# One loaded mask for all branches, an early read of the largest count, and a first gate unit that is split for crowded experts

## The chip, the cores and the metric

One core of a Trainium2 chip runs the whole program. The metric is device time in microseconds (us) of one launch. Engines: PE (TensorE, matmuls), DVE (VectorE), ACT (ScalarE), POOL (GpSimd), SP (here the issuer of the weight loads). Each runs its own instructions in order.

## The reference

Two post-norm layers over 256 positions of width 1024. Each layer has a mixer (spatial gating beside gated linear attention) and a feed-forward; the second layer's is a mixture of 8 experts, of which each position takes two.

```python
def gla_chunked(q, k, v, log_a):          # chunks of 64 positions, 4 heads
    ...
    scores = jnp.where(causal, jnp.einsum('nbhid,nbhjd->nbhij', q_dec, k_inv), 0.0)
    o_intra = jnp.einsum('nbhij,nbhje->nbhie', scores, v)
    ...
def swiglu(x, w_gate, w_up, w_down):
    return (jax.nn.silu(x @ w_gate) * (x @ w_up)) @ w_down

def moe_swiglu(x, w_router, e_gate, e_up, e_down):    # 8 experts, 1024 -> 3584 -> 1024
    logits = (t @ w_router).astype(jnp.float32)
    top_val, top_idx = lax.top_k(logits, TOP_K)
    top_w = jax.nn.softmax(top_val, axis=-1)
    gates = jnp.sum(jax.nn.one_hot(top_idx, N_EXPERTS, dtype=jnp.float32) * top_w[..., None], axis=1)
    out = jnp.zeros_like(t)
    for e in range(N_EXPERTS):
        out = out + gates[:, e:e + 1] * swiglu(t, e_gate[e], e_up[e], e_down[e])
```

All tensors are float32.

## The kernel before, in words

**Precision.** A float32 matmul is made of faster passes in F32R, a format with fewer bits that TensorE reads in one go: ACT copies an operand to its high part `h`, DVE subtracts to get the low part `l` (the helper `split`, lines 263 and 264). A product is `h·h + l·h + h·l`. A matmul of unsplit float32 operands needs no split, and takes two instructions in the trace for each one in the program.

**Weights.** Expert weights come as units of 1 MB: 128 partitions x 2048 float32. The loop over experts `e` takes columns in groups `g`, one of 512 and three of 1024 (group 3 is the last). A group of 1024 has four gate units `eg` (u0 to u3), four up units `eu`, and four down units `ed`, 12 loads. The class `Stream` keeps a ring of slots of one unit: a load takes a slot for `r`, a split takes two more for `h` and `l` and gives back `r`'s, and `free` gives back the rest once the product has read them. `tick()` stands for a step of the program's time: it lets the side tasks go on (a task that yields 4 goes on four ticks later) and pumps the stream, that is, issues the loads for which slots are free and the splits that are due. The order of each engine's instructions is the order in which this Python code emits them.

**Few and many.** Each expert gathers its positions into up to 128 columns. With 64 or fewer, the high parts stand in columns 0 to 63 and the low parts in 64 to 127, so that one pass does two, and the passes with `exl` or `cle` are left out. The choice is a branch on PE, ACT and DVE: `Expert.cases` (line 952) tests the expert's count, which `nc.values_load` (line 890) has read into a register of each of the three engines, once for each of the 8 experts. An expert with more than 64 positions is called a many expert below, the others few experts.

**The unsplit unit.** The first gate unit u0 of every group but the very first is not split. Its 4 matmuls (8 instructions, line 1033) multiply the raw weights `r` by `xw`, an unsplit copy of half of the gathered positions, for many and few experts alike. One `tick()` stands before each of the four.

**Side tasks that fall in this unit.** In the last group of an expert the next expert's gather starts: `one_hot` on DVE (lines 962 to 969), then four ticks, then `gather`: two transposes on PE (line 995), the first pick (8 matmuls in the program, line 983), its split `exh` (lines 974, 975), and two ticks later the second pick. In the second group of an expert the last one's `scatter` starts: two splits (`yh`, `yl`), three ticks, two pairs of matmuls (lines 1145, 1146) for the first half, two ticks, two pairs for the second half.

**Elsewhere.** In the mixer, the attention product of the first 128 positions is written as two matmuls of 64 columns for each head (line 640). At the end of the program, line 1226 reads the largest count of an expert, and line 1227 branches on it: a loop for counts over 128, which is jumped over here.

Of the kernel before, what the change touches and what calls it, by code (L numbers as in the profile page):

```python
# [8 lines left out]
F32 = mybir.dt.float32  # L9
# [30 lines left out]
def trunk(ctx: ExitStack, tc: tile.TileContext, x, w_in, gm_ws, gm_bs, gm_ln_g, gm_ln_b, gla_wa2, gla_ba,  # L40
# [86 lines left out]
    class Stream:  # L127


        def __init__(self):  # L130
            self.plan, self.index, self.parts, self.raw, self.held = [], {}, {}, {}, {}
            self.loaded = self.split = self.freed = 0
            self.whole = set()
# [5 lines left out]
        def add(self, key, src, a, b, pieces=1, ticks=4, whole=False):  # L139

            self.index[key] = len(self.plan)
            if whole:
                self.whole.add(self.index[key])
            self.plan.append((src, a, b, pieces, self.at))
            self.at += ticks

        def cols(self, key, w, c0, n, pieces=(1, 1), ticks=None, whole=()):
            v = w[:, c0:c0 + n].rearrange("(k p) n -> p k n", p=P)
            kk = 2048 // n
            for u in range(KT // kk):  # L150
                self.add((*key, u), v[:, u * kk:u * kk + kk, :], kk, n, pieces[u] if kk > 2 else 1, ticks or kk,
                         u in whole)
# [23 lines left out]
        def converting(self):  # L176
            i = self.split
            src, a, b, pieces, _ = self.plan[i]
            if i == self.loaded:
                self.load()  # L180
            r, slot = self.raw.pop(i)
            if i in self.whole:
                self.parts[i] = r, None
                self.held[i] = slot,
                self.split += 1
                return
            h, sh = self.slot(f"h{i}", F32R, a, b)
            l, sl = self.slot(f"l{i}", F32R, a, b)
# [275 lines left out]
    def mixer(l, xT, small, ready, nxT):  # L464
# [70 lines left out]
        def attention():  # L535
# [98 lines left out]
            for tb in range(2):  # L634
                yield 6
                po = psy(f"o{l}{tb}", (P, H, P))
                for h in range(H):
                    p, hh = divmod(h, 2)
                    for r in (slice(0, 64), slice(64, P)) if tb == 0 else (slice(0, P),):
                        nc.tensor.matmul(po[r, h, :], scT[tb][:, h, r], vs[tb][:, h * P:(h + 1) * P], start=True,  # L640
                                         stop=tb + r.start == 0)
                    for c in (2 * tb, 2 * tb + 1):
                        if c > 0:
                            r = slice(64 * (c % 2), 64 * (c % 2) + 64)
                            nc.tensor.matmul(po[r, h, :], qbd[tb][:, p, hh, r], S[c][:, p, :], start=False, stop=True)
# [136 lines left out]

    def moe_plan():
        prev = None
        for e in range(NE):
            for g, (c0, n) in enumerate(groups(e)):
                W.cols(("eg", e, g), exp_g[0, e], c0, n, ticks=4, whole=(0,) if e + g else ())
# [12 lines left out]
    def moe_constants():  # L800
# [9 lines left out]
        nc.vector.tensor_tensor(pair, ident[0:2 * NE, 0:NE], ident[0:2 * NE, NE:2 * NE], op=ALU.add)  # L810

        fold = const.tile([P, HALF], F32, name="fold")
        nc.vector.tensor_tensor(fold, ident[:, 0:HALF], ident[:, HALF:P], op=ALU.add)
        return iota, pri, one.to_broadcast([P, P]), ecst, pair, fold

    def moe(xT, ready, consts):
        iota, pri, ones, ecst, pair, fold = consts
# [33 lines left out]
        load_i = const.tile([P, NE], I32, name="load_i")  # L851
# [3 lines left out]
        def routing():  # L855
# [78 lines left out]
        class Expert:  # L934
# [7 lines left out]
            def __init__(self, nm, rank, gate, fewer=None):  # L942
                self.nm, self.rank, self.gate, self.fewer = nm, rank, gate, fewer
                self.load = None
                self.hT = {}

            def cases(self, few, many):

                if self.load is None:
# [41 lines left out]
            def gather(self):  # L991
# [9 lines left out]
                for hf in range(2):  # L1001
# [3 lines left out]
                    if hf == 0:  # L1005
                        if self.load is not None:
# [11 lines left out]
            def product(self, units, n, nm):  # L1018
# [6 lines left out]
                for u, ((wh, wl), free) in enumerate(units):  # L1025
                    held.append(free)
                    for j in range(kk):
                        k = kk * u + j
                        for b in range(nb):
                            s = slice(b * 512, b * 512 + 512)  # L1030
                            tick()
                            if wl is None:
                                nc.tensor.matmul(p[b], self.xw[:, k, :], wh[:, j, s], start=k == 0, stop=False,  # L1033
                                                 skip_group_check=True)
                                continue
# [13 lines left out]
                return p  # L1049

# [107 lines left out]


# [66 lines left out]
        most = nc.values_load(cnt_i[0:1, 0:1], min_val=0, max_val=2 * P)  # L1226
# [154 lines left out]
```

## Time and profile before

| | us |
|---|---|
| median of 3 runs | 1357.31 (1356.94 to 1363.91) |
| the profiled execution | 1356.93 |
| its span | 1355.2 |
| PE busy | 1295.6 (96%) |
| DVE busy | 1066.6 (79%) |
| ACT busy | 842.0 (62%) |
| DMA queue of the weights, share of 16 engines | 80.1% |

The span is what the trace covers, from its first instruction to its last; 1.7 us of the execution lie around it. A row of a timeline gives start, duration, engine, line, operation, output and inputs, and how many instructions it joins; in brackets the idle time of the engine before it and what ended that. PE and PEld are matmuls and weight loads of TensorE; a name with a q (PEldq, DVEq) is an engine's sequencer: loads of registers, branches, semaphores.

### The profile page before, as it was taken

The numbers are of one execution on the slowest core, as the hardware profiler recorded it, in microseconds if no ns is written. First come the engines' busy times: TensorE is split into PE (matmuls) and PEld (weight loads), VectorE is DVE, ScalarE is ACT, GpSimd is POOL, SyncE is SP. The second block draws the span as 40 slices with busy tenths as digits, with TensorE's granted clock in tenths as the row PEclk, the third lists the DMA queues.
The fourth block names the chain that finished last, engine by engine and source line by source line (L and its number), as shares of the span: only waits on it lengthen the run. The fifth ranks groups of instructions, "written<-read, shape, count | busy, mean of one in ns | idle before, by whom it ended". The sixth has DMA issues, their size and how long they took to land. (4 is left out here: it accounts for less than half of the span.)

```text
span 1355.2 us, 16887 instructions
## 1 busy us (share of the span) xinstructions
PE 1295.6 (96%) x6129; PEld 1035.2 (76%) x6129; DVE 1066.6 (79%) x963; ACT 842.0 (62%) x702; POOL 38.3 (3%) x71
## 2 busy tenths in 40 slices
PE   9999999999998999999999999999998999989895
PEld 7888888888886787787678778768776776877774
DVE  6687544386773888898977789799799989978887
ACT  5654444336432756787656668777677787767674
POOL 1012000000100000000000000000000000000000
PEclk9999999999998999999999999999999999999898
DMA  9646655444573599899999899999999999999993
GB/s 352 246 144 215 229 187 202 171 156 156 186 280 124 226 361 356 342 410 353 413 380 369 317 352 400 355 412 413 382 384 411 413 380 411 412 349 411 377 410 135
DMA packets 118765, 426.34 MB, mean 315 GB/s; under 512 B 8089, under 2 KB 10722, under 8 KB 104578
## 3 DMA queue, kind: packets, MB, share of 16 engines
q1 hardware_dynamic: 117218, 420.61, 80.1%
q0 software_dynamic: 1440, 4.33, 1.1%
q8 instruction: 64, 1.05, 0.3%
q14 instruction: 43, 0.35, 0.1%
HBM read 423.86 MB, written 1.05 MB: 314 GB/s over the span
## 5 line engine op out<-in xcount | busy, mean ns | idle before, releaser
L264 DVE TENSOR_TENSOR l<-r,h 128x2048 fp32r<-128x2048 f32 (+2 forms) x373 | 831.9, 2249 | 115.9 <-ACT h L263 102.0
L263 ACT ACTIVATE h<-r 128x2048 fp32r<-128x2048 f32 (+2 forms) x373 | 688.9, 1882 | 131.0 <-DVE l L264 31.6
L1118 PE MATMUL bank<-h,che 128*128 128x512 f32 x440 | 173.7, 395 | 0.0
L1036 PE MATMUL eu<-h,exh 128*128 128x512 f32 x440 | 167.4, 389 | 0.0
L1125 PE MATMUL bank<-l,che 128*128 128x512 f32 x377 | 147.5, 391 | 0.1
L1043 PE MATMUL eu<-l,exh 128*128 128x512 f32 x361 | 140.6, 389 | 0.4 <-DVE l L264 0.4
L1036 PE MATMUL eg<-h,exh 128*128 128x512 f32 x316 | 129.2, 421 | 0.0
L1033 PE MATMUL eg<-r,xw 128*128 128x512 f32 x248 | 121.4, 625 | 0.0
L1036 PEld LDWEIGHTS eu<-h,exh 128*128 128x128 f32 x440 | 82.6, 188 | 17.1
L1118 PEld LDWEIGHTS bank<-h,che 128*128 128x128 f32 x440 | 82.7, 188 | 16.5
L1043 PE MATMUL eg<-l,exh 128*128 128x512 f32 x237 | 92.8, 391 | 0.1
L1125 PEld LDWEIGHTS bank<-l,che 128*128 128x128 f32 x377 | 70.8, 188 | 15.5 <-DVE l L264 1.6
L1043 PEld LDWEIGHTS eu<-l,exh 128*128 128x128 f32 x361 | 67.8, 188 | 14.8 <-DVE l L264 0.8
L1033 PEld LDWEIGHTS eg<-r,xw 128*128 128x128 f32 x248 | 47.3, 199 | 41.0 <-issue 39.2
L1036 PEld LDWEIGHTS eg<-h,exh 128*128 128x128 f32 x316 | 59.9, 190 | 16.4 <-issue 5.0
L258 PE MATMUL f<-h,xhm 128*128 128x512 f32 (+1 forms) x192 | 72.1, 375 | 0.0
L260 PE MATMUL f<-h,xlm 128*128 128x512 f32 (+1 forms) x192 | 71.4, 372 | 0.0
L259 PE MATMUL f<-l,xhm 128*128 128x512 f32 (+1 forms) x192 | 71.4, 372 | 0.0
L1043 PEld LDWEIGHTS eg<-l,exh 128*128 128x128 f32 x237 | 44.8, 189 | 13.3 <-issue 3.4
L1089 PEld LDWEIGHTS bank<-fold,sge 128*128 128x128 f32 x336 | 45.0, 196 | 12.8 <-DVEq L952 7.2
L1089 PE MATMUL bank<-fold,sge 128*128 128x64 f32 x336 | 45.0, 277 | 4.4 <-DVEq L952 4.4
L1056 ACT ACTIVATE sge<-eg 128x512 f32<-128x512 f32 x55 | 30.1, 594 | 27.3 <-PE eg L1015 25.6
(351 smaller groups left out, 1789.6 us busy)
## 6 DMA issues: line engine op xcount, KB each, us to landing
r<-in_exp_w_gate SPq DMA_DIRECT2D x112, 1024.0 KB, 9.0
r<-in_exp_w_up SPq DMA_DIRECT2D x112, 1024.0 KB, 9.5
r<-in_exp_w_down SPq DMA_DIRECT2D x110, 1024.0 KB, 12.4
r<-in_w_in SPq DMA_DIRECT2D x17, 1024.0 KB, 8.3
r<-in_ffn_w_gate SPq DMA_DIRECT2D x11, 1024.0 KB, 6.8
r<-in_ffn_w_up SPq DMA_DIRECT2D x11, 1024.0 KB, 5.1
r<-in_ffn_w_down SPq DMA_DIRECT2D x11, 1024.0 KB, 4.9
r<-in_w_out SPq DMA_DIRECT2D x8, 1024.0 KB, 9.6
```

Source lines behind the costliest of these rows:

```text
L258: nc.tensor.matmul(ps, xh, wh, start=start, stop=False)
L259: nc.tensor.matmul(ps, xh, wl, start=False, stop=False)
L260: nc.tensor.matmul(ps, xl, wh, start=False, stop=stop)
L263: nc.scalar.activation(dst_h, src, AF.Copy)
L264: nc.vector.tensor_tensor(dst_l, src, dst_h.bitcast(F32), op=ALU.subtract)
L1033: nc.tensor.matmul(p[b], self.xw[:, k, :], wh[:, j, s], start=k == 0, stop=False, skip_group_check=True)
L1036: nc.tensor.matmul(p[b], xh[:, k, :], wh[:, j, s], start=k == 0, stop=False, skip_group_check=True)
L1043: nc.tensor.matmul(*second[0:3], start=False, stop=False, skip_group_check=True)
L1056: nc.scalar.activation(o, i, f)
L1089: nc.tensor.matmul(tp[:, j, i * HALF:i * HALF + HALF], hidden_columns(t, j), fold, start=True, stop=True)
L1118: nc.tensor.matmul(y, ch[:, k, :], wh[:, j, s], start=first and u + j == 0, stop=False, skip_group_check=True)
L1125: nc.tensor.matmul(y, ch[:, k, :], wl[:, j, s], start=False, stop=False, skip_group_check=True)
```

## The change

**One mask.** Three small DVE operations make one number whose bit `e` says whether expert `e` has over 64 positions. It is loaded once. A branch tests `mask & 2 ** e`: each one now has a REGISTER_ALU instruction ahead of its comparison. Eight memsets on POOL make the powers of two.

**The early read.** The load of the largest count moves from the end of the program to group 1 of expert 4. The branch on it stays.

**The unit u0.** For many experts it is split and used in three F32R passes (12 instructions), like the others; few experts use it raw as before (8 instructions). Both stand in branches, the split as well. The slots for `h` and `l` are taken whichever branch runs, so that u0 holds three slots where it held one; its four ticks all come ahead of its matmuls.

**The mixer.** The two 64-column matmuls become one of 128 columns.

```diff
             r, slot = self.raw.pop(i)
+            h, sh = self.slot(f"h{i}", F32R, a, b)
+            l, sl = self.slot(f"l{i}", F32R, a, b)
             if i in self.whole:
-                self.parts[i] = r, None
-                self.held[i] = slot,
+                self.whole[i](lambda: split(h, l, r))
+                self.parts[i] = h, l, r
+                self.held[i] = sh, sl, slot
                 self.split += 1
                 return
...
-                    for r in (slice(0, 64), slice(64, P)) if tb == 0 else (slice(0, P),):
-                        nc.tensor.matmul(po[r, h, :], scT[tb][:, h, r], vs[tb][:, h * P:(h + 1) * P], start=True,
-                                         stop=tb + r.start == 0)
+                    nc.tensor.matmul(po[:, h, :], scT[tb][:, h, :], vs[tb][:, h * P:(h + 1) * P], start=True,
+                                     stop=False, skip_group_check=True)
...
-            nc.vector.tensor_copy(load_i, pc)
+            nc.vector.scalar_tensor_tensor(bits, pc, HALF + 0.5, powers, op0=ALU.is_gt, op1=ALU.mult)
+            nc.vector.tensor_reduce(msum, bits, axis=AX.X, op=ALU.add)
+            nc.vector.tensor_copy(mask_i, msum)
             experts[0].one_hot()
+            mask = nc.values_load(mask_i[0:1, 0:1], engines=[ET.PE, ET.Activation, ET.DVE], min_val=0,
+                                  max_val=2 ** NE - 1)
             for e in range(NE):
-                experts[e].load = nc.values_load(load_i[0:1, e:e + 1], engines=[ET.PE, ET.Activation, ET.DVE],
-                                                 min_val=0, max_val=2 * P)
+                experts[e].wide = mask & 2 ** e
...
-                with tc.If(self.load > HALF) as c:
+                with tc.If(self.wide > 0) as c:
...
-                for u, ((wh, wl), free) in enumerate(units):
+                for u, ((wh, wl, *raw), free) in enumerate(units):
                     held.append(free)
+                    if raw:
+                        tick(kk * nb)
+                        self.whole_unit(p, kk, wh, wl, raw[0])
+                        continue
...
+            def whole_unit(self, p, kk, wh, wl, raw):
+                xh, xl = self.x
+                def run(*passes):
+                    for k in range(kk):
+                        for b in range(len(p)):
+                            for i, (x, w) in enumerate(passes):
+                                nc.tensor.matmul(p[b], x[:, k, :], w[:, k, b * 512:b * 512 + 512],
+                                                 start=k + i == 0, stop=False, skip_group_check=True)
+                self.cases(lambda: run((self.xw, raw)), lambda: run((xh, wh), (xh, wl), (xl, wh)))
...
+            wide_only[e] = lambda many, ex=experts[e]: ex.cases(skip, many)
...
+                if (e, g) == (NE // 2, 1):
+                    most = nc.values_load(cnt_i[0:1, 0:1], min_val=0, max_val=2 * P)
...
-        most = nc.values_load(cnt_i[0:1, 0:1], min_val=0, max_val=2 * P)
```

The order of the instructions changes on PE around u0. In the gather of expert 5, in the last group of expert 4, PE has before (`eg430` and `eg431` are the gate sums, `r255` is unit u0, `oh25` the one-hot matrix, `bank3` the PSUM bank of the transposes and of the second pick):

```order
L1089 MATMUL bank2_3524<-fold_3150,upe421_8108 128x64 x4
L1033 MATMUL eg430_8219<-r255_7984,xw4_7234 128x512
L1033 MATMUL eg431_8220<-r255_7984,xw4_7234 128x512
L1033 MATMUL eg430_8219<-r255_7984,xw4_7234 128x512
L995 MATMUL bank3_3525<-ident_81,oh25_8213 128x128 x2
L983 MATMUL bank2_3524<-oh5_8210,xin0_75 128x128
...
L952 COMPARE_AND_BRANCH
L952 UNCONDITIONAL_BRANCH x2
L1033 MATMUL eg431_8220<-r255_7984,xw4_7234 128x512
L1036 MATMUL eg430_8219<-h256_8130,exh4_7219 128x512
L1043 MATMUL eg430_8219<-l256_8131,exh4_7219 128x512
L983 MATMUL bank3_3525<-oh5_8210,xin0_75 128x128
```

and after, from the same place:

```order
L1114 MATMUL bank2_3464<-fold_3151,upe421_9621 128x64 x4
L1008 MATMUL bank3_3465<-ident_81,oh25_9757 128x128 x2
L996 MATMUL bank2_3464<-oh5_9754,xin0_75 128x128
...
L965 COMPARE_AND_BRANCH
L1072 MATMUL eg430_9763<-h255_9639,exh4_8398 128x512
L1072 MATMUL eg430_9763<-l255_9640,exh4_8398 128x512
L1072 MATMUL eg430_9763<-h255_9639,exl4_8399 128x512
...
L1072 MATMUL eg430_9763<-r255_9473,xw4_8419 128x512
L1072 MATMUL eg431_9764<-r255_9473,xw4_8419 128x512
...
L1049 MATMUL eg430_9763<-h256_9682,exh4_8398 128x512
L1056 MATMUL eg430_9763<-l256_9683,exh4_8398 128x512
L996 MATMUL bank3_3465<-oh5_9754,xin0_75 128x128
```

Three of the unit's four raw matmuls stood ahead of the transposes and one behind the first pick; now all of them stand between the first pick and the second, in one arm of a branch, with the 12 passes of the other arm beside them.

In the scatter of expert 3, in group 1 of expert 4, PE has before (`yh30` and `yl30` are the two parts of the first half of the sums):

```order
L1033 MATMUL eg410_7698<-r233_7434,xw4_7234 128x512
L1033 MATMUL eg411_7699<-r233_7434,xw4_7234 128x512
L1145 MATMUL bank3_3525<-yh30_7690,pt3_6178 128x512
L1146 MATMUL bank3_3525<-yl30_7691,pt3_6178 128x512
...
L1033 MATMUL eg410_7698<-r233_7434,xw4_7234 128x512
L1033 MATMUL eg411_7699<-r233_7434,xw4_7234 128x512
L1145 MATMUL bank3_3525<-yh31_7694,pt3_6178 128x512
```

and after:

```order
L1232 TENSOR_LOAD cnt_i_3159
L1170 MATMUL bank3_3465<-yh30_9052,pt3_7003 128x512
L1171 MATMUL bank3_3465<-yl30_9053,pt3_7003 128x512
...
L1072 MATMUL eg410_9074<-r233_8801,xw4_8419 128x512
L1072 MATMUL eg411_9075<-r233_8801,xw4_8419 128x512
...
L1170 MATMUL bank3_3465<-yh31_9056,pt3_7003 128x512
```

Two raw matmuls stood ahead of the first half and two between the halves; now none stands ahead and all four between. The load of the largest count stands here, too.

In the routing, PE has before (`pc` holds the counts, `e001` a gate sum of expert 0):

```order
L883 MATMUL pc_3310<-sel_3155,one_3144 128x8 x2
L890 TENSOR_LOAD load_i_3159
L890 ISA x2
...
L258 MATMUL e001_3299<-h61_3008,xhm11_3218 128x512
L259 MATMUL e001_3299<-l61_3009,xhm11_3218 128x512
L260 MATMUL e001_3299<-h61_3008,xlm11_3219 128x512
L995 MATMUL oht0_3425<-ident_81,oh20_3320 128x128 x2
```

and after:

```order
L890 MATMUL pc_3311<-sel_3156,one_3136 128x8 x2
L901 TENSOR_LOAD mask_i_3160
L901 ISA x2
L259 MATMUL e001_3300<-h61_3000,xhm11_3219 128x512
L260 MATMUL e001_3300<-l61_3001,xhm11_3219 128x512
L261 MATMUL e001_3300<-h61_3000,xlm11_3220 128x512
L1008 MATMUL oht0_3346<-ident_81,oh20_3325 128x128 x2
```

Eight loads, each with two register instructions, have become one between the counts and the next product.

## Rows read from the trace of the kernel before

**Rows 1.** Windows: stretch, length, busy PE, PEld, DVE, ACT, POOL, clock, DMA share, GB/s.
```profile
700.00:750.00 50.00, 50.00 (x231) 39.42 (x230) 37.72 (x30) 29.89 (x25) 0.00 (x0) 1.00 0.90 358
1000.00:1050.00 50.00, 46.40 (x197) 34.19 (x197) 46.48 (x31) 37.07 (x29) 0.00 (x0) 1.00 1.02 411
```
**Rows 2.** Instructions by line: count, min/median/max ns, first and last start.
```profile
L1015 PE MATMUL eu<-h,exl x104: 389/389/393, 450.1 to 763.3; 128*128 128x512 f32 x104
L1066 ACT ACTIVATE upe<-eu x42: 572/599/625, 546.4 to 1323.7; 128x512 f32<-128x512 f32 x42
```
**Rows 3.** The weight loads' issues from 955 to 967 us, then from 975 to 990.
```profile
DMA to landing us min/median/max: 10.7/12.6/14.5
...
DMA to landing us min/median/max: 5.1/6.9/7.1
```
**Rows 4.** Timeline at 410.3 us, the routing.
```profile
417.07 0.79 PE L258 MATMUL e<-h,xhm 128*128 128x512 f32 x1 [6.05 <-issue]
```
**Rows 5.** The register instructions of line 890 on PE's sequencer.
```profile
L890 PEldq FUSED_REGOPS  x8: 146/146/160, 411.9 to 416.8; - x8
```
**Rows 6.** Line 640, the mixer's product, both layers.
```profile
L640 PE MATMUL o<-v,scT x48: 271/273/377, 67.4 to 354.7; 128*64 128x128 f32 x32, 128*128 128x128 f32 x16
```
**Rows 7.** PE's timeline: F32R passes, a raw unit, and what follows.
```profile
699.99 1.98 PE L1015 MATMUL bank<-h,cle 128*128 128x512 f32 x8
702.03 3.59 PE L1033 MATMUL eg<-r,xw 128*128 128x512 f32 x8
705.46 0.63 PE L1098 MATMUL bank<-ident,sge 128*128 128x128 f32 x4
```
**Rows 8.** The two operations of a split, by line and form.
```profile
L264 DVE TENSOR_TENSOR l<-r,h 128x2048 fp32r<-128x2048 f32 x361 | 819.9, 2289 | 115.3 <-ACT h L263 101.5 <-DVEq L952 2.7 <-issue 2.3
L263 ACT ACTIVATE h<-r 128x2048 fp32r<-128x2048 f32 x361 | 678.5, 1914 | 127.6 <-DVE l L264 31.6 <-DMA r<-in_exp_w_gate 27.2 <-PE eg L1015 13.9
```
**Rows 9.** Timeline of a gather in a few expert's last group.
```profile
963.18 2.79 PE L1033 MATMUL eg<-r,xw 128*128 128x512 f32 x6
967.58 0.43 PE L995 MATMUL bank<-ident,oh 128*128 128x128 f32 x2 [1.60 <-DVE oh L969]
968.89 2.66 PE L983 MATMUL bank<-oh,xin 128*128 128x128 f32 x16 [0.88 <-DVE che L1094]
971.34 1.92 PE L1033 MATMUL eg<-r,xw 128*128 128x512 f32 x2
973.74 1.95 PE L983 MATMUL bank<-oh,xin 128*128 128x128 f32 x16
976.14 0.42 DVE L975 TENSOR_TENSOR exh<-bank,exh 128x256 fp32r<-128x256 f32 x1 [3.71 <-ACT exh L974]
980.26 0.38 SPq L169 DMA_DIRECT2D r<-in_exp_w_gate  x1
```
**Rows 10.** Timeline of a gather in a many expert's last group.
```profile
737.42 2.74 PE L1033 MATMUL eg<-r,xw 128*128 128x512 f32 x6
740.38 2.02 PE L983 MATMUL bank<-oh,xin 128*128 128x128 f32 x16
742.24 1.02 PE L1033 MATMUL eg<-r,xw 128*128 128x512 f32 x2
```
**Rows 11.** Timeline of a scatter, in group 1 of expert 4.
```profile
906.12 1.88 PE L1033 MATMUL eg<-r,xw 128*128 128x512 f32 x4
910.67 0.50 PE L1146 MATMUL bank<-yl,pt 128*128 128x512 f32 x1 [2.44 <-DVE yl L264]
```
**Rows 12.** Line 952 and, at the end of the program, line 1227 on PE's sequencer.
```profile
L952 PEldq COMPARE_BRANCH  x382: 65/202/338, 418.5 to 1336.5; - x191
...
L1227 PEldq COMPARE_BRANCH  x1: 3796/3796/3796, 1341.0 to 1341.0; - x1
```
**Rows 13.** DVE's load of the largest count, and the operation that waits behind the branch.
```profile
L1226 DVEq TENSOR_LOAD <-cnt_i x1: 317/317/317, 1341.4 to 1341.4; - x1
...
1344.72 0.16 DVE L1276 TENSOR_TENSOR mean<-total 128x2 f32<-128x2 f32 x1 [2.52 <-DVEq L1227]
```

More of the change, by code (lines that the diff above doesn't have):

```diff
@@ L132, in __init__ @@
             self.loaded = self.split = self.freed = 0
-            self.whole = set()
+            self.whole = {}
             self.hold = False
@@ L137, in __init__, with add, cols @@
             self.lead, self.reserve = 12, NR
-        def add(self, key, src, a, b, pieces=1, ticks=4, whole=False):
+        def add(self, key, src, a, b, pieces=1, ticks=4, whole=None):
             self.index[key] = len(self.plan)
             if whole:
-                self.whole.add(self.index[key])
+                self.whole[self.index[key]] = whole
             self.plan.append((src, a, b, pieces, self.at))
             self.at += ticks
-        def cols(self, key, w, c0, n, pieces=(1, 1), ticks=None, whole=()):
+        def cols(self, key, w, c0, n, pieces=(1, 1), ticks=None, whole=None):
             v = w[:, c0:c0 + n].rearrange("(k p) n -> p k n", p=P)
@@ L151, in cols @@
                 self.add((*key, u), v[:, u * kk:u * kk + kk, :], kk, n, pieces[u] if kk > 2 else 1, ticks or kk,
-                         u in whole)
+                         None if u else whole)
         def rows(self, key, w, r0, ticks=4, pieces=1, order="(k p) n -> p k n"):
@@ L644, in attention @@
                             r = slice(64 * (c % 2), 64 * (c % 2) + 64)
-                            nc.tensor.matmul(po[r, h, :], qbd[tb][:, p, hh, r], S[c][:, p, :], start=False, stop=True)
+                            nc.tensor.matmul(po[r, h, :], qbd[tb][:, p, hh, r], S[c][:, p, :], start=False, stop=True,
+                                             skip_group_check=True)
                 sq = s2(f"sq{l}{tb}", F32, (P, H, P))
@@ L781, in trunk @@
     PAIRS = "(p k) n -> p k n"
+    wide_only = {}
     def moe_plan():
@@ L786, in moe_plan @@
             for g, (c0, n) in enumerate(groups(e)):
-                W.cols(("eg", e, g), exp_g[0, e], c0, n, ticks=4, whole=(0,) if e + g else ())
+                W.cols(("eg", e, g), exp_g[0, e], c0, n, ticks=4,
+                       whole=(lambda many, e=e: wide_only[e](many)) if e + g else None)
                 W.cols(("eu", e, g), exp_u[0, e], c0, n, ticks=4)
@@ L810, in moe_constants @@
         nc.vector.tensor_tensor(pair, ident[0:2 * NE, 0:NE], ident[0:2 * NE, NE:2 * NE], op=ALU.add)
+        powers = const.tile([P, NE], F32, name="powers")
+        for e in range(NE):
+            nc.gpsimd.memset(powers[:, e:e + 1], float(2 ** e))
         fold = const.tile([P, HALF], F32, name="fold")
         nc.vector.tensor_tensor(fold, ident[:, 0:HALF], ident[:, HALF:P], op=ALU.add)
-        return iota, pri, one.to_broadcast([P, P]), ecst, pair, fold
+        return iota, pri, one.to_broadcast([P, P]), ecst, pair, fold, powers
     def moe(xT, ready, consts):
-        iota, pri, ones, ecst, pair, fold = consts
+        iota, pri, ones, ecst, pair, fold, powers = consts
         lg = const.tile([P, 2, NE], F32, name="lg")
@@ L1005, in gather @@
                     if hf == 0:
-                        if self.load is not None:
+                        if self.wide is not None:
                             self.xw = room[-1].tile([P, 4, P], F32, tag="xw", name=f"xw{nm}", bufs=2)
@@ L1031, in product @@
                             tick()
[L1032 to L1035, printed above, removed]
                             nc.tensor.matmul(p[b], xh[:, k, :], wh[:, j, s], start=k == 0, stop=False,
@@ L1157, in moe, with skip @@
                           small[:, e:e + 1]) for e in range(NE)]
+        def skip():
+            pass
+        for e in range(NE):
+            wide_only[e] = lambda many, ex=experts[e]: ex.cases(skip, many)
         pgs = {}
```

10 lines of the change are left out of this document (5 added, 5 removed).

## The prediction

> **What bounds the kernel now.** I read the windows of the expert stage first, then the counts by line, the weight loads' issues, and last the timelines at the places where the order of PE's instructions changes. The windows show two regimes [rows 1]. In 700 to 750 us PE is busy for all 50.00 us, DVE for 37.72 and ACT for 29.89, and the DMA share is 0.90: PE sets the pace. In 1000 to 1050 us PE is busy for 46.40 us, DVE for 46.48, and the DMA share is 1.02 at 411 GB/s. A unit of 128 x 2048 float32 is 1.049 MB, so a load takes 1.049/411 = 2.55 us, and nearly all of the time is that: the loads set the pace, as long as slots come back in time. The counts tell which expert is in which regime [rows 2]. Line 1015 with `exl`, a pass of the many arm alone, runs 104 times for the up sums: 14 units of 4 give 56 in a whole expert, and 48 in expert 0, whose first group is computed elsewhere; 104 is 56 + 48, two experts, all before 763.3 us. The `upe` copies of the few arm run 42 times, 7 in each of the other six. So experts 0 and 2 are many, the rest few.
>
> In the few regime the loads are queued: they land 10.7 to 14.5 us after issue, median 12.6 [rows 3]. Behind a gather they land after 5.1 us at the least, so the queue has run empty there. The timeline shows why [rows 9]: DVE stands 3.71 us until 976.14, for an `exh` that needs the second pick (973.74 on PE); the splits that give slots back are behind it, and the next weight load is issued at 980.26. What delays the second pick delays the loads of an expert that is paced by loads.
>
> **The change part by part.**
>
> *(a) The routing.* PE idles 6.05 us before 417.07 [rows 4] while its sequencer reads eight counts: the register instruction behind a load starts at 411.9 for the first and at 416.8 for the last [rows 5], 4.9 us for seven loads, 0.70 each. These go. The one that stays waits for two small DVE operations more, 0.16 us each by the small one at the end of the program [rows 13], and with their waits on each other some 0.5 (an estimate). I take -4.9 + 0.5 = -4.4. The ends are -5.6 (all but the one load of the 6.05) and -1 (the gather's one-hot, which is behind the same DVE operations, ends the idle time instead).
>
> *(b) The mixer.* Line 640 has 48 instructions, 32 of them with 64 columns [rows 6]; two become one, so 16 go. Their median duration, 273 ns, overlaps with the next; issue in that stretch goes on at some 0.10 us, an estimate from the 128-column pass rate: 16 in 1.95 us at 973.74, that is 0.12 [rows 9]. 16 x 0.105 = -1.7. The ends are 0 (the next operation waits for another input) and -4.4 (16 x 0.273).
>
> *(c) The unit of a many expert.* A raw unit takes 705.46 - 702.03 = 3.43 us [rows 7]; nine F32R passes take 702.03 - 699.99 = 2.04, 0.227 each. Twelve are 2.72: -0.71 a unit. There are 7 such units (3 in expert 0, 4 in expert 2). Two of them hold gathers and one a scatter, costed below. Of the other four, the two of expert 0 I take at nothing, since the stream there is just starting and `h` and `l` come from slots that other loads want: by the order in which slots are taken, two loads of its group 2 go out 16 to 20 ticks later. Two in expert 2 are paid: -1.4. Each adds a split, 2.29 us on DVE and 1.91 on ACT [rows 8]; it lies under PE, since DVE has 50.00 - 37.72 = 12.3 us free in 50 [rows 1]. Without that cover the two would cost 2 x 2.29 = +4.6. The ends are -5.0 (all seven) and +4.6.
>
> *(d) Two gathers in a many expert.* The order puts all of the unit between the two picks. Before, 6 of the 8 raw instructions stood ahead of the transposes and filled PE while DVE prepared its inputs from 737.42 on [rows 10]; the first pick starts at 740.38, when DVE has freed its bank, and 2 stood behind it. What moves ahead cannot start the pick earlier, so PE idles there, and behind it come 2.72 us in place of 2 x 0.43 = 0.86: +1.86 each, +3.7 in all. The ends are 0 (the pick moves up by as much) and 2 x 2.57 = +5.1 (six raw instructions of 0.429).
>
> *(e) Five gathers in a few expert* (in experts 1, 3, 4, 5, 6). As in (d), but the unit stays raw: 6 instructions change sides, 6 x 0.429 = 2.57 us. The transposes wait for DVE's `oh` until 967.58, with 1.60 idle, and the pick for `che`, with 0.88 [rows 9]; both are DVE's times and come no earlier. The six that ran from 963.18 on leave an idle engine, and the second pick comes at 973.74 + 2.57. DVE's `exh`, now idle 3.71 ahead of 976.14, waits 2.57 more, and so do the splits and the load at 980.26. As that load found an empty queue, the delay is lost: 5 x 2.57 = +12.9. The ends are 0 (the queue holds enough after all) and 5 x 3.43 = +17.2 (the whole unit).
>
> *(f) Seven scatters.* Before, 4 raw instructions ran ahead of the first half, from 906.12, and 4 behind it; the second half of its sums waits for `yl` until 910.67, with 2.44 idle [rows 11]. Now none is ahead, PE idles from 906.12 on, and the 4 come later: 4 x 0.429 = 1.72 at most, 7 x 1.72 = 12.0 in all. Here DVE waits little for PE, and the loads in front of it are queued for 10.7 us and more [rows 3], so most of it stays hidden. I take 1.5, a little under one of the seven; the ends are 0 and 12.0. If that cover is gone, it is the price of the third rival.
>
> *(g) The end.* DVE's 1276 waits until 1344.72 behind the branch, 2.52 us [rows 13]; its load of the count, about 0.3 us there, goes: -0.3. The branch itself, 3.80 us on PE's sequencer [rows 12], stays. In the middle of the program the load stands ahead of a scatter's matmuls, which wait for `yl` longer than the 0.70 us that a load takes. If nothing hid it, it would be +0.7, and without a saving at the end 0.
>
> *(h) Edits at nothing.* REGISTER_ALU ahead of every branch: 382 compare-and-branch instructions run on PE's sequencer, 202 ns in the median [rows 12], 77 us in all, in a stage where PE is busy for 50.00 of 50 [rows 1]. The sequencer runs ahead of the array and hides them. The nearest row for the added one is a register operation of 0.146 us [rows 5]: uncovered, 382 x 0.146 = +56. The 8 memsets run on POOL, which is idle there. The slots: u0 holds three for a while, so that by the order in which slots are taken 5 of the 12 loads of a group go out 7 or 8 ticks later; a tick is three passes, 0.68 us, so about 5.3 us. The queue holds 12.6 - 5.1 = 7.5 us [rows 3], more than that: 0. Uncovered it is one load of 2.55 us at each of the five gathers, +12.8. Neither of these can gain.
>
> The sum: -4.4 - 1.7 - 1.4 + 3.7 + 12.9 + 1.5 - 0.3 = +10.3. The profiled execution took 1356.93 us, 1355.2 of it the span; it lies 0.4 below the median of 1357.31. 1356.9 + 10.3 = 1367.2.
>
> **The rivals.**
>
> *R1, the queue absorbs the gathers (faster).* The mechanism is the stock of queued loads: if at each gather the loads issued so far keep the DMA busy until the late one is issued, (d) to (f) cost nothing, and -4.4 - 1.7 - 1.4 - 0.3 = -7.8 is left: 1349.1, and 1345.5 if all seven units of (c) are paid. It decides where the last load issued before the gather lands later than the first one after it is issued. For it: 12.6 us of queue. Against it: 5.1 us behind the gather, an empty queue.
>
> *R2, half of it.* DVE and the queue make up for half of (e) and (d), say: +6.4 + 1.9 - 7.8 = +0.5, 1357.4. For it: DVE catches up after a gather, with 3.5 us free in 50 [rows 1]. Against it: the loads have no such room.
>
> *R3, the scatters in full.* PE's 1.72 us in each scatter count, since ACT's and DVE's splits stand behind `yl` and the loads behind them: 12.0 in place of 1.5, 1377.7. For it: 2.44 idle at 910.67. Against it: no empty queue shows there.
>
> *R4, code is fetched at each new branch.* At the end of the program one taken branch over a long loop takes 3.80 us [rows 12]. If the 24 new branches into the few arm on PE did the same, that is 24 x 3.80 = +91: 1458. Against it: the branches of line 952 take 202 ns and at the most 338. The Trainium skill, "Runtime: NRT & Kernel Launch", section "Instruction fetch mechanics", says that a taken branch whose target is outside the fetched window forces a fetch before execution goes on; by that rule the far branch of line 1227 pays and the near ones do not, and the trace agrees with 3.80 us against 0.20. The new arms are 12 instructions long.
>
> **How the numbers follow.** Forecast 0.50, with a range of its own from 1362 to 1373 (the scatters at 0 to 4, and (e) at 9 to 17); R1 0.17; R2 0.15; R3 0.15; R4 0.03. What this kernel's measurement can tell from no change is about 0.5%, 6.8 us: 1350.5 to 1364.1. Faster is R1 but for 0.02 of it: 0.15. Same is R2, that 0.02, and 0.06 from the lower edge of the forecast: 0.23. Slower is the rest, 0.44 + 0.15 + 0.03 = 0.62. The range of 8 in 10 reaches from 1349 (the middle of R1) to 1382 (R3 and some of the late loads).
>
> **What would show it.** PE's idle time before the first product behind the counts should fall from 6.05 to about 1.6 us. In the few gathers the transposes should wait over 4 us for `oh`, the whole unit should stand between the picks, DVE should wait over 6 us for the second `exh`, and the next load should land after some 5 us. Each of the last groups of experts 1, 3, 4, 5 and 6 should be 2.6 us longer than before, and the others not. In experts 0 and 2 the unit should take 2.72 us. I am wrong if the loads behind a gather are not late, or if the loads of a whole group are late because u0 holds its slots.

## The result and the profile after

The changed kernel takes 1421.5 us (median of 6 runs) against 1358.66 for the kernel before (also 6 runs): ratio 1.046, 95% interval 1.0442 to 1.0478, some 63 us slower. The forecast was 1367.2 with a range up to 1382. The sign was right, the size six times too small. The profiled execution has a span of 1423.8 us.

The windows of the changed kernel, with the columns of [rows 1]:

```profile
700.00:750.00 50.00, 50.00 (x228) 41.56 (x227) 42.08 (x24) 36.32 (x25) 0.00 (x0) 1.00 0.96 381
1000.00:1050.00 50.00, 46.37 (x211) 36.27 (x211) 37.82 (x32) 31.76 (x27) 0.00 (x0) 0.93 0.83 329
```

With the many experts PE is as full as before. The windows from 1000 to 1050 us cannot be set against each other: the changed kernel runs later, and its window begins with a gather, which before lay at 967.58. So I take the same work in both, from the transposes of expert 5's gather to those of expert 6's: 111.7 us before, 123.0 now. The bytes did not change: 395 GB/s over 111.67 us are 44.1 MB, 360 over 123.00 are 44.3. DVE's busy time did not change either (99.12 and 99.09). The DMA share fell from 0.99 to 0.91, so the DMA stood still for longer; PE is busy 3.8 us longer, at a granted clock of 0.94 for 0.98, and idle 7.5 us longer. Before, then after:

```profile
967.58:1079.25 111.67, 104.96 (x491) 82.17 (x491) 99.12 (x75) 82.17 (x65) 0.00 (x0) 0.98 0.99 395
```

```profile
1002.41:1125.41 123.00, 108.75 (x490) 83.99 (x491) 99.09 (x75) 83.09 (x65) 0.00 (x0) 0.94 0.91 360
```

The gather in expert 4's last group, on PE, in the changed kernel [rows 9 of before]:

```profile
1002.41 0.66 PE L1008 MATMUL bank<-ident,oh 128*128 128x128 f32 x2 [5.45 <-DVE oh L982]
1003.73 3.63 PE L996 MATMUL bank<-oh,xin 128*128 128x128 f32 x16 [0.66 <-DVE che L1119]
1007.19 3.60 PE L1072 MATMUL eg<-r,xw 128*128 128x512 f32 x8
1011.08 1.95 PE L996 MATMUL bank<-oh,xin 128*128 128x128 f32 x16
```

The transposes wait 5.45 us for `oh` instead of 1.60; the whole unit of 8 instructions stands between the picks; the second pick begins 8.67 us after the transposes instead of 6.16, which is 2.51 later, as the prediction's 2.57. What it did not have is the clock: after the idle 5.45 us, the first pick takes 3.63 us. The window over transposes and first pick shows a granted clock of 0.50, 1.2 GHz:

```profile
1002.40:1007.00 4.60, 3.93 (x17) 3.60 (x18) 3.31 (x5) 0.38 (x1) 0.00 (x0) 0.50 1.03 422
```

DVE waits 5.25 us for the second `exh`, and the loads wait with it. First DVE, then the issues of down loads from 990 to 1010 us and from 1010 to 1020 (columns as [rows 2]):

```profile
1013.48 0.42 DVE L988 TENSOR_TENSOR exh<-bank,exh 128x256 fp32r<-128x256 f32 x1 [5.25 <-ACT exh L987]
```

```profile
L169 SPq DMA_DIRECT2D r<-in_exp_w_down x2: 341/362/384, 1001.1 to 1001.5; - x2
...
L169 SPq DMA_DIRECT2D r<-in_exp_w_down x2: 328/376/424, 1017.6 to 1018.0; - x2
```

Before, all four down loads of that group were out at 966.6, ahead of the transposes, and only the next gate load (980.26) came behind the gather. Now two are out at 1001.5; the other two wait for the splits behind the gather and go from 1017.6 on. The loads that had been queued run out before that: from 1011 to 1018 us the DMA share is 0.00.

```profile
1011.00:1018.00 7.00, 7.00 (x41) 6.08 (x40) 3.14 (x3) 4.94 (x4) 0.00 (x0) 1.00 0.00 0
```

The 9 us behind the gather, before and after:

```profile
976.00:985.00 9.00, 9.00 (x41) 7.46 (x40) 7.39 (x5) 9.00 (x8) 0.00 (x0) 1.00 0.76 281
```

```profile
1011.00:1020.00 9.00, 9.00 (x50) 7.73 (x49) 5.05 (x4) 6.94 (x7) 0.00 (x0) 1.00 0.15 40
```

A DMA share of 0.15 where it was 0.76: 5.5 us lost in this one place. PE is busy for all 9.00 us of both, with weights that had been split by then; it idles elsewhere in the expert (7.5 us more in the two windows above).

### The profile page after: what moved, and what is told of

It reads as the page before. It is cut to its first block, busy times and chain, and to the rows that moved or that the text cites. A ratio compares the mean times of both kernels' runs of the same rounds, so it can differ in the third digit from the quotient of the medians.

```text
span 1423.8 us, 18228 instructions
## 1 busy us (share of the span) xinstructions
PE 1318.7 (93%) x6141; PEld 1055.5 (74%) x6141; DVE 1080.1 (76%) x972; ACT 859.2 (60%) x709; POOL 37.6 (3%) x79
## 5 line engine op out<-in xcount | busy, mean ns | idle before, releaser
L265 DVE TENSOR_TENSOR l<-r,h 128x2048 fp32r<-128x2048 f32 (+2 forms) x380 | 847.7, 2250 | 144.0 <-ACT h L264 134.3
L264 ACT ACTIVATE h<-r 128x2048 fp32r<-128x2048 f32 (+2 forms) x380 | 705.7, 1883 | 222.5 <-DMA r<-in_exp_w_gate 40.4
L1150 PE MATMUL bank<-l,che 128*128 128x512 f32 x377 | 150.7, 400 | 1.3 <-DVE l L265 0.2
L1072 PE MATMUL eg<-r,xw 128*128 128x512 f32 x192 | 95.7, 645 | 0.0
L1072 PEld LDWEIGHTS eg<-r,xw 128*128 128x128 f32 x192 | 39.6, 212 | 41.3 <-issue 40.0
L1114 PE MATMUL bank<-fold,upe 128*128 128x64 f32 x336 | 47.2, 284 | 0.0
```

What stands on the lines that cost most here:

```text
L264: nc.scalar.activation(dst_h, src, AF.Copy)
L265: nc.vector.tensor_tensor(dst_l, src, dst_h.bitcast(F32), op=ALU.subtract)
L1072: nc.tensor.matmul(p[b], x[:, k, :], w[:, k, b * 512:b * 512 + 512], start=k + i == 0, stop=False, skip_group_check=True)
L1114: nc.tensor.matmul(tp[:, j, i * HALF:i * HALF + HALF], hidden_columns(t, j), fold, start=True, stop=True)
L1150: nc.tensor.matmul(y, ch[:, k, :], wl[:, j, s], start=False, stop=False, skip_group_check=True)
```

## The experiments

Four theories were on the table. S: the two further slots that u0 holds make loads late. O: the order of the ticks. T: only both together. B: the register instruction ahead of every branch.

**e1, the order alone.**

```diff
-                    for j in range(kk):
+                    if wl is None:
+                        tick(kk * nb)
+                    for j in range(kk):
...
-                            tick()
+                            if wl is not None:
+                                tick()
```

> The kernel before, with the four ticks of unit u0 ahead of its four raw matmuls and nothing else of the change; the slots stay as they were. The changed kernel took 1421.5 us, 62.8 over before; with the 6.4 that routing, mixer and end were to save, some 69 are to be explained. Theory S (the two further slots that u0 holds make loads late): this kernel pays only the prediction's terms for gathers and scatters, +10 to +17, 1368 to 1375 us. Rival O (the order of the ticks does it): +45 or more, 1403 us and up. Rival T (neither alone, both together): +5 to +17, 1363 to 1375 us. Rival B (the register instruction ahead of each branch): +10 to +17.

Measured: ratio 1.0252 (1.0216 to 1.0288), +34 us. More than S and less than O expected: neither range holds, and the order costs about half of the loss. The gather in expert 4 has the change's picture: transposes behind 4.31 us of idle time, the first pick at half clock (0.52 over both), and the next load at 1004.11, 14.96 us after the transposes (12.68 before).

```profile
989.15 0.66 PE L995 MATMUL bank<-ident,oh 128*128 128x128 f32 x2 [4.31 <-DVE oh L969]
990.47 3.39 PE L983 MATMUL bank<-oh,xin 128*128 128x128 f32 x16 [0.66 <-DVE che L1097]
```

**e2, the slots alone.**

```diff
-                self.held[i] = slot,
+                self.held[i] = idle.pop(0), idle.pop(0), slot
```

> The kernel before, with two idle slots taken when u0 is due and held until u0's own is freed; they are not used, and the order of PE's instructions is as it was. Theory S: +40 to +60, 1398 to 1418 us, with loads issued late behind the split of u0 and an empty DMA queue at each gather. Rival O: under +12, below 1370 us. Rival T: under +20, below 1378 us. Rival B: 0 to +12.

Measured: 1.0284 (1.0246 to 1.0322), +38.6 us. The slots alone, unused, cost the other half, a little under S's range; O and T, with at most 20, are far off. The prediction had 0 for them. PE's order is as before; the two late down loads are there all the same. SP's timeline joins the issues that follow each other on one tensor:

```profile
986.12 15.44 SPq L169 DMA_DIRECT2D r<-in_exp_w_down  x4
1001.61 4.11 SPq L169 DMA_DIRECT2D r<-in_exp_w_gate  x2
```

The gathers are not all of it. I added up the idle time of the DMA, in windows of 1 us, over the 30 us from each gather's transposes on and from each scatter's first product on. Behind the seven gathers it is 26 us before and 53 in e2, behind the seven scatters 9 before and 23 in e2: +27 and +14, about the price. One scatter (expert 4's), before and in e2:

```profile
1019.50:1049.50 30.00, 26.40 (x111) 19.50 (x111) 28.55 (x18) 21.37 (x17) 0.00 (x0) 1.00 1.02 411
1043.36:1073.36 30.00, 27.42 (x104) 19.89 (x104) 25.18 (x17) 20.04 (x15) 0.00 (x0) 0.89 0.92 363
```

The clock falls here too, though the order of PE's instructions is that of before: the transposes wait 2.88 us for `oh`, and over them and the first pick the granted clock is 0.50.

```profile
987.48:992.30 4.82, 4.17 (x18) 3.82 (x19) 3.30 (x5) 0.38 (x1) 0.00 (x0) 0.50 1.04 424
```

**e3, both,** with the two edits above.

> The kernel before with both: the four ticks first and the two slots held. No mask, no split branch, no mixer edit. Theory S and rivals O and T: +65 to +75, 1423 to 1433 us, since what is missing of the change is only its small parts. Rival B: +10 to +30, below 1388 us, since most of the loss is then with the branches.

Measured: 1.0512 (1.0476 to 1.0548), +69.7. The sum of the two alone is 72.9, so they add, with at most a few us of overlap. S and O each held half of the cause; T and B are out. This kernel has none of the small parts and is slower than the whole change.

**e4, the mask alone.**

```diff
...
-                experts[e].load = nc.values_load(load_i[0:1, e:e + 1], engines=[ET.PE, ET.Activation, ET.DVE],
-                                                 min_val=0, max_val=2 * P)
+                experts[e].load = mask & 2 ** e
...
-                with tc.If(self.load > HALF) as c:
+                with tc.If(self.load > 0) as c:
```

> The kernel before with the one mask: three small DVE operations, one load for each engine in place of eight, and the register instruction ahead of all branches. Theory S and rivals O and T: -4.4 (-5.6 to -1), 1354 us, and PE's idle time ahead of the first product behind the counts 1.6 us in place of 6.05. Rival B: +30 or more, 1388 us and up.

Measured: 0.9976 (0.9958 to 0.9994), -3.3 us. The register instructions ahead of PE's 382 branches do not show in the time; each takes 36 ns on PE's sequencer, and the prediction's price without cover was 56 us in all. From the counts to the transposes it is 418.51 - 410.43 = 8.08 us before and 416.84 - 413.20 = 3.64 here, -4.4 as predicted, and the wait is 1.60. Before, then e4:

```profile
410.43 0.59 PE L883 MATMUL pc<-sel,one 128*128 128x8 f32 x4
418.51 0.63 PE L995 MATMUL oht<-ident,oh 128*128 128x128 f32 x2
```

```profile
413.20 0.59 PE L887 MATMUL pc<-sel,one 128*128 128x8 f32 x4
415.40 0.79 PE L258 MATMUL e<-h,xhm 128*128 128x512 f32 x1 [1.60 <-DVE slot L976]
416.84 0.63 PE L1004 MATMUL oht<-ident,oh 128*128 128x128 f32 x2
```

**e5 and e6, the slots by group.** The same two slots, held only where the group is in a list: 1 and 3 in e5, as below, 0 and 2 in e6.

```diff
+                if key[2] in (1, 3):
+                    self.more.add(self.index[key])
...
-                self.held[i] = slot,
+                self.held[i] = (idle.pop(0), idle.pop(0), slot) if i in self.more else (slot,)
```

> The kernel before, with the two slots held as in the run of all slots (1.0284 of before, +38.6 us), but only in groups 1 and 3, where the scatters and the gathers fall. Theory D (a late load costs only where DVE stands still and the queue runs empty, which is at gathers and scatters): +32 to +40, 1392 to 1400 us. Rival U (fewer slots slow every group alike): half of it, +19, some 1379 us.

> The same in groups 0 and 2 alone, where no gather and no scatter falls. Theory D: 0 to +6, below 1367 us. Rival U: +19, some 1379 us.

Measured: groups 1 and 3 cost 1.0297 (1.0272 to 1.0322), +40, all of it; groups 0 and 2 cost 1.0119 (1.0092 to 1.0146), +16. U is out for groups 1 and 3, where D holds. In groups 0 and 2 D fails, which had 6 at the most, and U's 19 lies within the interval. The two prices do not add up: 40 and 16, against 38.6 for all groups. Why is not shown. In e6 the last two down loads leave ahead of the gather, as before. Some 6 of its 16 us lie at the gathers all the same: the next gate load goes out later behind the transposes than before, 6.4 us in the sum of the seven, and in expert 4 the granted clock over transposes and first pick is 0.51 behind 2.06 us of idle time. Where the rest lies was not found. e5 holds gathers and scatters together; what parts them is the DMA's idle time under e2.

```profile
982.94 15.43 SPq L172 DMA_DIRECT2D r<-in_exp_w_down  x4
```

```profile
977.40 0.80 SPq L172 DMA_DIRECT2D r<-in_exp_w_down  x2
```

The first is e5: four down loads over 15.43 us, the gather between the second and the third. The second is e6: the last two, 0.80 us, ahead of the gather.

**e7, the change with the unit in four branches,** a tick ahead of each.

```diff
-                        tick(kk * nb)
                         self.whole_unit(p, kk, wh, wl, raw[0])
...
+                for k in range(kk):
+                    for b in range(len(p)):
+                        tick()
+                        self.cases(lambda: run(k, b, (self.xw, raw)),
+                                   lambda: run(k, b, (xh, wh), (xh, wl), (xl, wh)))
```

> The changed kernel with the unit in four branches, one for each of its four steps, and a tick ahead of each, so that gathers and scatters stand where they stood before. All the rest of the change stays, slots too. If the order of the ticks costs what it cost alone (1.0252, +34 us), this is 34 below the changed kernel: 1384 to 1392 us. Rival (a branch in the middle of the matmuls costs, 93 more of them on PE): 1400 us and up.

Measured: 1.0269 (1.0244 to 1.0294), 1397.0 us. By the two ratios that is 26 us below the changed kernel, not 34, between the two expectations. The order is given back, the slots stay, and what is left, +36.6, is near the slots' price of e2. Whether the missing 8 us are the 93 branches or an overlap of the two causes, no run here tells; the clock over transposes and first pick is 0.50 here as well, behind 2.85 us of idle time, and it is not given back.

**e8, the mixer alone.**

```diff
-                    for r in (slice(0, 64), slice(64, P)) if tb == 0 else (slice(0, P),):
-                        nc.tensor.matmul(po[r, h, :], scT[tb][:, h, r], ...
+                    nc.tensor.matmul(po[:, h, :], scT[tb][:, h, :], ...
```

> The kernel before with the mixer's edit alone. The prediction's term: the block of products of the first 128 positions, from the first of line 640 to the first matmul behind it (67.41 to 69.31 us before, 1.90), shrinks to 1.0 to 1.1 us in each layer, -1.7 in all. Rival P (two 64-column matmuls run beside each other, and a change between 64 and 128 columns costs): the block grows to 3.0 us, +1.1 in each layer, +2.2 in all.

In the trace of one run the block goes from 69.31 - 67.41 = 1.90 us to 70.71 - 67.69 = 3.02, as rival P had it. The time of one run is too little for a verdict; the changed kernel's trace has the same block in 71.08 - 68.06 = 3.02 us. Before:

```profile
67.41 0.54 PE L640 MATMUL o<-v,scT 128*64 128x128 f32 x5
67.79 0.27 PE L640 MATMUL o<-v,scT 128*64 128x128 f32 x1
67.80 0.27 PE L645 MATMUL o<-S,qbd 128*64 128x128 f32 x1
69.31 0.50 PE L258 MATMUL og<-h,xhin 128*128 128x512 f32 x1
```

and in e8, where 128- and 64-column products alternate:

```profile
67.69 0.38 PE L639 MATMUL o<-v,scT 128*128 128x128 f32 x2
68.00 0.43 PE L644 MATMUL o<-S,qbd 128*64 128x128 f32 x2
68.37 0.49 PE L639 MATMUL o<-v,scT 128*128 128x128 f32 x2
68.78 0.43 PE L644 MATMUL o<-S,qbd 128*64 128x128 f32 x2
70.71 0.50 PE L258 MATMUL og<-h,xhin 128*128 128x512 f32 x1
```

Before, two 64-column products on different halves start 0.01 us apart and both take 0.27 us: they run beside each other. The term was to be -1.7 and is +1.1 in each of two layers.

**e9 and e13, the order by group.** As e1, with the ticks ahead of the unit only in group 1, where the scatters are, or only in group 3, where the gathers are.

```diff
+                    early = wl is None and nm[3:4] == "1"
+                    if early:
+                        tick(kk * nb)
...
-                            tick()
+                            if not early:
+                                tick()
```

> The kernel before, with the four ticks ahead of the unit only in group 1 of each expert, where the scatters fall; the gathers stay as they were. All groups together cost +34 us (1.0252). In that run the next load after a scatter was issued 10.97 us after the one before it, in place of 8.12, so 2.85 late. Theory D (a scatter's delay reaches the loads in full): 7 x 2.85 = +20, some 1379 us, and the gathers have the other 14. The prediction's term: +1.5. Rival F (only PE's 1.72 us a scatter count): +12, 1371 us.

> The kernel before, with the four ticks ahead of the unit only in group 3 of each expert, where the gathers fall. All groups together cost 1.0252 (+34 us), group 1 alone 1.0033 (+4.5). Theory G (the gathers have the rest, more than their 2.57 us of moved instructions each): +25 to +31, 1385 to 1392 us. Rival H (the gathers cost what the prediction gave them, +16.6, and the rest is in groups 0 and 2, where no side task starts): +14 to +18, 1374 to 1379 us.

Measured: group 1 1.0033 (1.0019 to 1.0048), +4.5 us for seven scatters; group 3 1.0189 (1.016 to 1.0218), +25.7 for seven gathers, 3.7 each. For the scatters D (20) and F (12) are wrong, and the prediction's 1.5 is below the interval, 2.6 to 6.5 us. For the gathers G is right. Together they are 30 of the 34. In e13 the granted clock over transposes and first pick is 0.50 again:

```profile
980.70:985.80 5.10, 4.39 (x19) 4.08 (x20) 3.35 (x5) 0.38 (x1) 0.00 (x0) 0.50 1.03 422
```

The gather in expert 4 of e13, to be read beside [rows 9], and the next gate load:

```profile
980.75 0.66 PE L995 MATMUL bank<-ident,oh 128*128 128x128 f32 x2 [4.63 <-DVE oh L969]
982.06 3.76 PE L983 MATMUL bank<-oh,xin 128*128 128x128 f32 x16 [0.66 <-DVE che L1098]
985.61 4.75 PE L1037 MATMUL eg<-r,xw 128*128 128x512 f32 x8
990.65 1.95 PE L983 MATMUL bank<-oh,xin 128*128 128x128 f32 x16
997.18 0.38 SPq L169 DMA_DIRECT2D r<-in_exp_w_gate  x1
```

The load goes out 16.43 us after the transposes, 12.68 before. Over the seven gathers this lateness is 3.0 to 4.3 us each and 25.2 in sum; the second pick's is 25.2 too. So the delay of the second pick reaches the loads in full, and its sum is close to the measured 25.7.

**e14, one slot.**

```diff
-                self.held[i] = slot,
+                self.held[i] = idle.pop(0), slot
```

> The kernel before, with one further slot held with u0 in place of two (two: 1.0284, +38.6 us). If the loss grows with the lateness of the loads: about half, +15 to +23, 1375 to 1383 us. If the queue has room for one slot and the second alone empties it: below +8, 1368 us. If one slot is enough to push the two last down loads of group 3 behind the gather: +30 or more, 1390 us.

Measured: 1.0086 (1.0057 to 1.0115), +11.7 us, between the first and the second case, with an interval (8 to 16) that reaches into the first: under half of what two cost. Now three of the four down loads are joined in SP's row, and one of them is behind the gather:

```profile
971.51 15.30 SPq L169 DMA_DIRECT2D r<-in_exp_w_down  x3
```

Down loads behind the gather and DMA share in the 9 us there: none and 0.76 before, none and 0.65 in e6, one and 0.33 in e14, two and 0.22 in e2. The time follows: 0, +16, +11.7, +38.6, with e6 out of line.

**e10, e11 and e12, what is left over.** e10 is the mask and the early read. e11 takes out the two ticks between a gather's picks; e12 also sets the scatter two ticks later, behind all of the raw unit.

```diff
                             nc.scalar.activation(self.xw, p, AF.Copy)
-                        yield 2
...
                     yp.append((yh, yl))
-                yield 3
+                yield 5
```

> The kernel before with the mask and the early read alone: no mixer edit, the unit u0 as before. From the mask alone (0.9976) and the trace of its routing: -3 to -5 us, 1354 to 1356, ratio 0.9963 to 0.998. If the early read costs, 1.000.

> As the mask and the early read, and the second pick of a gather directly behind the first: two raw instructions and two F32R passes, 2 x 0.43 + 2 x 0.23 = 1.3 us, go behind it. Theory D (at a gather the queue is dry, and the loads hang on the second pick): the opposite of the change, 1.3 to 2.4 us a gather in the five few gathers, -6 to -12 against the mask and the read alone, 1343 to 1349 us. Rival A (DVE and ACT need the time between the picks, the second only waits longer): no gain, 1354 to 1356.

> As the one with the picks together, and the scatter's first half two ticks later: all four raw matmuls of unit u0 stand ahead of it, none between the halves. Theory D: the opposite of the order that cost some 20 us in the seven scatters; PE's idle time ahead of the first half (2.4 us) takes two raw matmuls, 1.7 us, so 0 to -10 against the one with the picks together. Rival A: DVE's sums wait for PE longer, and the loads with them: +5 to +15.

Measured: e10 0.9974 (0.9958 to 0.9989); e11 0.9943 (0.9921 to 0.9964), 1353.4 us; e12 0.9927 (0.9912 to 0.9942), 1351.6 us, the fastest, 9.4 below before. The early read shows neither gain nor loss beside e4's 0.9976. e11's step of 4.7 us has the sign of D and less than its 6 to 12, and its interval overlaps e10's, so the time alone does not show it. The trace has its sign: the DMA share in the 9 us behind expert 4's gather is 0.98, against 0.76 before and 0.50 in e10, and DVE's wait is 1.36:

```profile
968.00:977.00 9.00, 9.00 (x40) 7.32 (x39) 7.53 (x5) 8.62 (x7) 0.00 (x0) 1.00 0.98 389
```

```profile
967.90 0.42 DVE L984 TENSOR_TENSOR exh<-bank,exh 128x256 fp32r<-128x256 f32 x1 [1.36 <-ACT exh L983]
```

e12 cannot be told from e11, but from e10 it can. The 20 us for the scatters from which e12's theory D starts were themselves a forecast; e9 puts them at 4.5.

## Why the prediction was wrong

The step that failed most is (h), *the slots at nothing*. It set a lateness of 5.3 us against a stock of 7.5, both in time. Two mistakes stand in that. The 5.3 us were ticks at the pace of a running PE; in the last group the ticks contain the gather, at which DVE stands for 5 us, so a load that is two places further back in the slots' order goes out behind it, 16 us after the one ahead (1001.5 to 1017.6). And the 7.5 us were the depth of the queue on average, while at the gather it was empty already [rows 3]: the rows that (e) used against R1 spoke against this cover too. Measured: +38.6 where the term was 0 and its upper end 12.8. That end counted the five few gathers alone; about a third of the price is at the scatters, by the DMA's idle time under e2. The prediction's own last sign of being wrong, loads late because u0 holds its slots, came true. The other half of (h) held: the register instructions cost nothing (e4).

Steps (d) and (e), *the gathers*, had the mechanism and the moved instructions right (2.51 us against 2.57) and the size too small: 25.7 for the seven against 16.6. e13 has the raw unit in all seven, so 7 x 2.57 = 18.0 of its 25.2 us of delay are the moved instructions. What the sum left out is the clock: in expert 4 PE idles 4.63 us ahead of the transposes, and then works at 1.2 GHz through them and the first pick, 3.76 us for the sixteen instead of 2.66. Over the seven gathers the first picks take 23.8 us instead of 18.3, 5.5 longer. The remaining 1.7 are not assigned; the raw unit behind the pick is slower as well in expert 4, 4.75 us against 3.59 [rows 7]. The sign that DVE waits over 6 us for the second `exh` did not come in the changed kernel's gather (5.25), since the delay is shared: the wait for the first `exh` grew too, from 1.06 to 2.02 us.

Step (f), *the scatters*, was 1.5 and is 4.5. The cover that it counted on, loads queued for 10.7 us and more, is thinner once the slots are held: behind the seven scatters the DMA idles 34 us in the changed kernel and 9 before. A scatter's raw unit also runs at a lower clock there, behind waits of 3.31 and 2.89 us: 0.61 in the mean, and the row of its eight instructions is 5.51 us long against 3.59 [rows 7]:

```profile
1059.84 0.49 PE L1170 MATMUL bank<-yh,pt 128*128 128x512 f32 x1 [3.31 <-ACT yh L264]
1064.67 5.51 PE L1072 MATMUL eg<-r,xw 128*128 128x512 f32 x8
```

Step (a), the routing, was right at -4.4. Step (b), the mixer, had the wrong sign, since it priced 64-column products one after another; its 0.105 us is also not what the row behind it gives (1.95 / 16 = 0.12). Step (c) cannot be separated: e3, with neither split nor small parts, is at 1.0512, the change at 1.046; 7 us lie between, of which routing and mixer explain 4.4 - 2.2 = 2.2, and the intervals are 2 to 5 us to either side. The many unit itself takes the 12 passes it was to take, 760.96 - 758.13 = 2.83 us in expert 2's gather (2.72 predicted). In (g) DVE's wait behind the branch is 0.16 us here against 2.52 [rows 13], but it has only moved: two operations later DVE waits 1.93 us for the same branch on PE, which still takes 3.84. In e4, with the load at its old place, the two waits are 0.28 and 2.08. So the branch, not the read, holds DVE.

```profile
1413.86 2.08 DVE L1315 SCALAR_TENSOR_TENSOR y<-acc,mean,gb 128x512 f32<-128x512 f32 x3 [1.93 <-PEq L1259]
```

Of the rivals, R1 and R2 fell with the empty queue. R4 fell with the changed kernel's trace: its 458 compare-and-branch instructions of line 965 on PE, the new ones among them, take 373 ns at the most. R3 priced the scatters at 12; alone they cost 4.5, and the late loads stood only at the upper end of (h).

| part | predicted | measured | by |
|---|---|---|---|
| two slots held by u0 | 0 | +38.6 | e2 |
| gathers, order | +16.6 | +25.7 | e13 |
| scatters, order | +1.5 | +4.5 | e9 |
| routing | -4.4 | -4.4 (trace), -3.3 (time) | e4 |
| mixer | -1.7 | +2.2 (trace) | e8 |
| whole change | +10.3 | +63 | the changed kernel |

## What to carry to other kernels

Before you take a buffer that is held longer as free, read the depth of the queue at its shallowest point (the load that lands soonest after issue), not at the median: here it was 5.1 us against 12.6, and one slot cost 11.7 us, two 38.6. Then look at which loads change sides of the nearest stall: a load that slips behind a stalled engine is late by the whole stall, not by the few steps it was moved. A filler that is moved away from a wait cost twice here, once as the work that now stands behind the wait (18.0 us) and once as the clock that the idle time took from the work after it (5.5 us in the first picks).

## What the hardware showed that was not expected

Two float32 products of 64 columns on the two halves of the array start 0.01 us apart and take 0.27 us each (67.79, 67.80); in e8, with a change between 128 and 64 columns behind every two products, two take 0.31 to 0.41 us from start to start (67.69, 68.00, 68.37, 68.78), and the block has eight such changes, the one at its end counted. The Trainium skill, "TensorEngine Tiling (Array Packing)", section "Key Properties", says that tiles work independently and that a change of the tiling drains the engine; by that rule the merged product loses the pair and pays the changes, and the trace agrees with 3.02 us against 1.90. How the 1.1 us divide between the two is not shown.

TensorE's granted clock was 0.50 to 0.52 over the transposes and first pick of expert 4 behind 4.3 to 5.5 us of idle time (e1, e13, the changed kernel), and also behind 2.88 us in e2, 2.85 in e7 and 2.06 in e6. It was 0.84 where the idle time ahead of them was 1.60, in the kernel before:

```profile
967.50:971.30 3.80, 2.84 (x18) 2.71 (x19) 3.38 (x5) 0.38 (x1) 0.00 (x0) 0.84 1.03 417
```

So in this kernel what fills a wait, or makes it longer, also decided at which clock the work behind it ran.
